# The first block's meta-token work and the last rows' normalization of a hybrid DeltaNet and attention layer, rewritten

## The chip, the cores and the metric

The kernel runs on one core of one Trainium2 chip. Its time is device microseconds (us) of one launch, and a kernel's time is the median of its runs. TensorE (PE in rows) does the matmuls; VectorE (DVE), ScalarE (ACT) and GpSimd (POOL) do elementwise work; SyncE (SP) issues nearly all transfers, in the order in which they are written. Each engine executes its own list of instructions in order and waits on semaphores for the others.

## What is computed

One layer over 2048 tokens of width 1024, preceded by 16 learned meta tokens. Cut to what matters:

```python
h = concatenate([meta, x], axis=1)
q_a, k_a, v_a, z_a, beta_a, dec_a, q_b, k_b, v_b, z_b, gate_a, gate_b = split(h @ w_in)
# branch A: gated DeltaNet, 8 heads of 128, chunks of 64
q, k, v = silu(causal_conv4(concat([q_a, k_a, v_a])))        # 4 taps a channel
beta = sigmoid(beta_a);  g = -exp(a_log) * softplus(dec_a + dt_bias)
lower = strict_tril(k_beta @ k.T * decay)
sol = triangular_solve(lower + eye, [v_beta, k_beta * exp(g_cum)])   # per chunk and head
S = S * exp(g_last) + k_dec.T @ (u - w @ S)                  # state carried over chunks
# branch B: sliding-window attention, 16 heads of 64, meta tokens always visible
mixed = sigmoid(gate_a) * (y_a @ w_proj_a) + sigmoid(gate_b) * (y_b @ w_proj_b)
out = layer_norm(alpha * x + mixed @ w_out)                  # rows of the 16 meta tokens dropped
```

## The kernel before

The 2048 tokens are four blocks of 512. A block runs through a fixed list of projections with weights of 128 output columns (a "unit", 24 matmuls of 128x512, `proj`, line 296), and between the pieces of six matmuls a loop (`run`) draws the next step of two side streams: the DeltaNet stages of the head groups and the attention. What an engine executes, and in which order, is so decided when the program is built, by counting those pieces ("ticks"); steps put off with `bg` come a written number of ticks later. On the chip each engine then goes through its list as soon as the semaphores allow.

Each fp32 matrix is split into a high part (rounded by ScalarE, line 261) and a low part (raw minus high, `split_lo`, line 144), and three products are summed. From the second block on, many high and low parts are read back from a DRAM copy that the first block wrote (`ws`), so the splitting is mostly work of block 0.

The eight DeltaNet heads run in four groups of two (g0 to g3). For each group and chunk the triangular system is inverted in two levels. The 32x32 diagonal blocks are inverted column by column on GpSimd: 31 columns of two instructions each (lines 812 and 814), on `X`, with `g` the transposed lower matrix. SP then stores `X` (line 820), loads it transposed as `XT` (line 825), GpSimd copies it into place (line 828), and TensorE's first matmuls that need it are those of line 890 (`XN`), which join the blocks. The four groups do this one after another; SP's list holds the store of `X` between the stores of weight parts (line 283) and the loads of the next weights (line 248).

In block 0 alone the 16 meta tokens run along: `meta_tok` makes their gates with `gates_math`, a second call of it beside that of the block's tokens; `meta_heads` gives each group its start state. It convolves the meta tokens' keys and values with four taps (`meta_conv`, lines 403 and 405), and inverts a 16x16 matrix per head, 15 columns of two instructions on two partitions (lines 472 and 474). All of this is on VectorE. The inversion stands in the same stretch of the program as the columns of lines 812 and 814.

Attention (`ls`, `mn`: lines 1077 to 1110) follows the DeltaNet groups. The last block ends with the output projection and, row tile by row tile (four of 128 tokens), with `sums` (line 1303: residual plus PSUM), `stats` (line 1306) and `norm_row`: line 1287 aggregates mean and variance, `rsqrt_small` (lines 160 to 166) makes the root with three Newton steps of three instructions, ScalarE applies it (line 1293), and weight and bias are applied on GpSimd, for the last row tile on VectorE (lines 1297 and 1298).

## Time and profile before

| | |
|---|---|
| median of 3 runs | 2669.69 us (2668.91 to 2675.93) |
| the profiled execution | 2665.94 us |
| its span, first to last instruction | 2664.2 us |
| mean granted TensorE clock | 0.994 |
| PE busy | 2600.1 us (98%) |
| DVE busy | 1587.5 us (60%) |
| ACT busy | 1223.7 us (46%) |
| POOL busy | 765.8 us (29%) |
| DMA, mean over the span | 173 GB/s |

Busy time is a sum over an engine's instructions. TensorE is busy nearly all the time, so the few stretches in which it waits, and what stands before its first and behind its last matmul, are what is left beside the matmuls themselves. All rows below are of the profiled execution, whose time is 1.74 us above its span.

### The profile page before, as it was taken

To read this page: it belongs to the slowest core of one execution; us is meant where nothing else is said; L and a number is where in the kernel's file an instruction comes from. 1 tells how busy PE (TensorE), PEld (TensorE's weight loads), DVE (VectorE), ACT (ScalarE), POOL (GpSimd) and SP (SyncE) were. 2 spreads that over 40 slices of the span, in tenths; PEclk is the share of its full clock that TensorE was granted. 3 is DMA by queue.
4 is the path that set the end of the run, shared out by engine and by line. 5 is a ranking of instruction groups with operands and counts; after the bars stand their busy time and mean duration, and the time that the engine had idled before them with its cause. 6 is when DMAs were issued, how large, how long until landed. Compare 5 with 4: busy or idle time off the path is not lost.

```text
span 2664.2 us, 44181 instructions
## 1 busy us (share of the span) xinstructions
PE 2600.1 (98%) x15308; PEld 2180.1 (82%) x15308; DVE 1587.5 (60%) x4041; ACT 1223.7 (46%) x3250; POOL 765.8 (29%) x1703
## 2 busy tenths in 40 slices
PE   8999999999999999999999999999999999999997
PEld 7677778888888888888887888888888788888885
DVE  6879758743565655762465564774347466476336
ACT  4556546542244545662224553664223455465422
POOL 2544324432055430111116433110103644011022
PEclk9999999999999999999999999999999999999998
DMA  7654555643574454664466445575357544567533
GB/s 256 203 175 165 186 193 187 197 164 97 196 250 147 144 168 149 206 196 142 152 219 194 147 138 159 179 210 179 114 165 247 158 146 149 159 193 213 166 95 126
DMA packets 243376, 461.64 MB, mean 173 GB/s; under 512 B 77993, under 2 KB 136001, under 8 KB 243153
## 3 DMA queue, kind: packets, MB, share of 16 engines
q1 hardware_dynamic: 243152, 458.82, 54.2%
q8 instruction: 121, 1.98, 0.3%
q14 instruction: 103, 0.84, 0.1%
HBM read 379.89 MB, written 78.82 MB: 172 GB/s over the span
## 4 chain that ended last, share of the span: by engine, by line
PE 81%; DVE 10%; DMA 3%; POOL 2%; ACT 2%; issue 1%; SPq 1%; DVEq 0%; POOLq 0%; ACTq 0%
PE acc L296 57%; PE ps L1110 2%; DVE s L689 2%; PE ps L1075 2%; PE ps L962 1%; PE ps L941 1%; PE ps L949 1%; PE ps L951 1%; PE ps L930 1%; PE ps L1128 1%; PE acc L1367 1%; PE acc L1370 1%; PE acc L1369 1%; PE ps L841 1%; POOL X L814 1%
## 5 line engine op out<-in xcount | busy, mean ns | idle before, releaser
L296 PE MATMUL acc<-xh,wh 128*128 128x512 f32 x1800 | 738.0, 410 | 1.7 <-ACT wh L261 1.7
L296 PE MATMUL acc<-xl,wh 128*128 128x512 f32 x1800 | 709.4, 394 | 0.0
L296 PE MATMUL acc<-xh,wl 128*128 128x512 f32 x1800 | 476.2, 396 | 0.0
L296 PEld LDWEIGHTS acc<-xh,wh 128*128 128x128 f32 x1800 | 341.2, 190 | 62.3 <-ACT wh L261 2.4
L296 PEld LDWEIGHTS acc<-xl,wh 128*128 128x128 f32 x1800 | 342.0, 190 | 58.1
L296 PEld LDWEIGHTS acc<-xh,wl 128*128 128x128 f32 x1800 | 331.2, 189 | 67.3 <-issue 0.5
L261 ACT ACTIVATE wh<-wr 128x1024 fp32r<-128x1024 f32 (+1 forms) x245 | 258.0, 1053 | 276.0 <-PE acc L296 162.9
L689 DVE SCALAR_TENSOR_TENSOR s<-st,cw,s 128x512 f32<-128x512 f32 x288 | 233.4, 810 | 66.6 <-ACT st L684 59.5
L144 DVE TENSOR_TENSOR wl<-wr,wh 128x1024 fp32r<-128x1024 f32 (+2 forms) x125 | 162.0, 1296 | 156.5 <-ACT wh L261 137.5
L296 PE MATMUL acc<-y,wh 128*128 128x512 f32 x1024 | 250.1, 392 | 0.0
L812 POOL TENSOR_TENSOR tm<-X,g 128x60 f32<-128x60 f32 (+24 forms) x496 | 167.3, 337 | 268.8 <-DMA g<-d 233.4
L296 PEld LDWEIGHTS acc<-y,wh 128*128 128x128 f32 x1024 | 189.1, 188 | 37.3
L296 PE MATMUL acc<-xh,wr 128*128 128x512 f32 x624 | 209.0, 402 | 0.0
L1227 POOL TENSOR_TENSOR g<-g 128x512 f32<-128x512 f32 x32 | 69.9, 2183 | 432.7 <-DVE g L1220 432.7
L814 POOL TENSOR_TENSOR X<-X,tm 128x60 f32<-128x60 f32 (+24 forms) x496 | 165.4, 333 | 38.9
L1220 DVE SCALAR_TENSOR_TENSOR g<-g,acc 128x512 f32<-128x512 f32 x64 | 44.0, 688 | 203.3 <-PE acc L296 203.1
L1056 POOL TENSOR_TENSOR g<-mo,slp 128x32 f32<-128x32 f32 x128 | 41.0, 330 | 389.7 <-DVE mn L1077 365.3
L1112 ACT ACTIVATE s<-ps 104x512 fp32r<-104x512 f32 (+2 forms) x128 | 76.4, 597 | 146.6 <-PE ps L1110 145.6
L296 PEld LDWEIGHTS acc<-xh,wr 128*128 128x128 f32 x624 | 116.2, 188 | 23.0
L1211 ACT ACTIVATE g<-acc,bg__157 128x512 f32<-128x512 f32 x64 | 44.1, 689 | 190.3 <-PE acc L296 189.7
L296 PE MATMUL acc<-y,wl 128*128 128x512 f32 x512 | 129.2, 391 | 0.0
L731 POOL TENSOR_TENSOR g<-cm,gh 128x256 fp32r<-128x256 f32 x64 | 50.7, 822 | 257.8 <-DVE gh L643 211.5
(327 smaller groups left out, 4761.5 us busy)
## 6 DMA issues: line engine op xcount, KB each, us to landing
wr<-in_wfm_dram SPq DMA_DIRECT2D x214, 512.0 KB
wl<-ws SPq DMA_DIRECT2D x165, 512.0 KB
wr<-ws SPq DMA_DIRECT2D x78, 512.0 KB
wh<-ws SPq DMA_DIRECT2D x75, 512.0 KB
ws<-wl SPq DMA_DIRECT2D x68, 512.0 KB
g<-kd SPq DMA_DIRECT2D x240, 96.0 KB
ws<-wh SPq DMA_DIRECT2D x38, 512.0 KB
wr<-in_wo_dram SPq DMA_DIRECT2D x32, 512.0 KB
```

Of the source, the lines that this page charges most:

```text
L144: eng.tensor_tensor(out=out_, in0=src, in1=f(hi), op=ALU.subtract)
L261: A.activation(hi, raw, AF.Copy)
L296: T.matmul(ps, w_[:, k, :], r_(k), start=(n == 0), stop=(n == 3 * NK - 1))
L689: V.scalar_tensor_tensor(out=acc, in0=st[:, 3 - d:TB + 3 - d], scalar=cw[:, s, 3 - d:4 - d], in1=acc, op0=ALU.mult, op1=ALU.add)
L731: G.tensor_tensor(out=gt[:, hh, c:c + 2], in0=tri.unsqueeze(1).to_broadcast([P, 2, P]), in1=part[:, c:c + 2, h0 + hh:h0 + hh + 1].to_broad ...
L812: G.tensor_tensor(out=tm[:, :n, :r], in0=X[:, :n, j:j + 1].to_broadcast([P, n, r]), in1=L[:, j:j + 1, j + 1:].to_broadcast([P, n, r]), op= ...
L814: G.tensor_tensor(out=X[:, :n, j + 1:], in0=X[:, :n, j + 1:], in1=tm[:, :n, :r], op=ALU.add)
L1075: T.matmul(o_, d["q", rt][:, 2 * cp2 + ch], KX[:, l, ch, s:208], start=l == 0, stop=l == 1)
L1110: T.transpose(out=pT[0:kt, j * 256 + rt * P:j * 256 + rt * P + P], in_=Pt[:, ch, rt, s + j * kt:s + j * kt + kt], identity=ident)
L1112: A.activation(ph[0:kt], pT[0:kt], AF.Copy)
L1211: A.activation(gt_[u][:, br, :], ps, AF.Tanh, scale=0.5, bias=bg_[:, 8 * br + u:8 * br + u + 1])
L1227: G.tensor_tensor(out=m[:, u % 2, :], in0=t[:, 0, :], in1=t[:, 1, :], op=ALU.add)
```

## The change

Five things are rewritten; what is computed stays the same.

- The gates of the meta tokens become a fifth column of the block's gate tile in block 0: one call of `gates_math` on five columns takes the place of two calls. Its polynomial takes 9 instructions in place of 17, in all blocks.
- The four taps of the meta tokens (7 instructions a call, 8 calls) and their inversion columns (30 instructions a group) go from VectorE to GpSimd.
- A low part that GpSimd makes (30 in block 0) is made in four pieces of 128x256.
- The first tile of x and the first weights are loaded and rounded in two pieces each.
- Roots: `rsqrt_col`, for one value per partition, takes two instructions a Newton step, with the operands as per-partition scalars. `norm_row` gives GpSimd fewer columns from row tile to row tile, and VectorE the others in two fused instructions; the last row tile's second half is multiplied by the weight before the root is there.

```diff
@@ -140,8 +140,11 @@
 
     f = lambda ap: ap.bitcast(F32)
     def split_lo(out_, src, hi, pool=False):
-        eng = G if pool else V
-        eng.tensor_tensor(out=out_, in0=src, in1=f(hi), op=ALU.subtract)
+        if not pool:
+            V.tensor_tensor(out=out_, in0=src, in1=f(hi), op=ALU.subtract)
+            return
+        for k in range(0, NK, 2):
+            G.tensor_tensor(out=out_[:, k:k + 2], in0=src[:, k:k + 2], in1=f(hi[:, k:k + 2]), op=ALU.subtract)
 
     S = [cp.tile([P, 2, P], F32, name=f"S{g}") for g in range(4)]
     carry = cp.tile([P, 24, 3], F32, name="carry")
...
@@ -153,17 +156,27 @@
-    def rsqrt_small(dst, x, shp, tag):
-        hx = tiny(shp, tag + "h")
+    def rsqrt_seed(dst, x, shp, tag):
         it = tp.tile(shp, I32, tag=tag + "i", name=nm(tag + "i"))
-        t = tiny(shp, tag + "t")
         V.tensor_scalar(out=it, in0=x.bitcast(I32), scalar1=1, scalar2=None, op0=ALU.logical_shift_right)
         V.tensor_scalar(out=dst.bitcast(I32), in0=it, scalar1=-1.0, scalar2=MAGIC, op0=ALU.mult, op1=ALU.add)
+        return tiny(shp, tag + "t")
+
+    def rsqrt_small(dst, x, shp, tag):
+        t = rsqrt_seed(dst, x, shp, tag)
+        for _ in range(3):
+            V.scalar_tensor_tensor(out=t, in0=x, scalar=-0.5, in1=dst, op0=ALU.mult, op1=ALU.mult)
+            V.tensor_tensor(out=t, in0=t, in1=dst, op=ALU.mult)
+            V.scalar_tensor_tensor(out=dst, in0=t, scalar=1.5, in1=dst, op0=ALU.add, op1=ALU.mult)
+
+    def rsqrt_col(dst, x, tag):
+
+        t = rsqrt_seed(dst, x, [P, 1], tag)
+        hx = tiny([P, 1], tag + "h")
         V.tensor_scalar(out=hx, in0=x, scalar1=-0.5, scalar2=None, op0=ALU.mult)
         for _ in range(3):
-            V.tensor_tensor(out=t, in0=dst, in1=dst, op=ALU.mult)
-            V.tensor_tensor(out=t, in0=t, in1=hx, op=ALU.mult)
-            V.scalar_tensor_tensor(out=dst, in0=t, scalar=1.5, in1=dst, op0=ALU.add, op1=ALU.mult)
+            V.tensor_scalar(out=t, in0=dst, scalar1=dst, scalar2=hx, op0=ALU.mult, op1=ALU.mult)
+            V.tensor_scalar(out=dst, in0=t, scalar1=1.5, scalar2=dst, op0=ALU.add, op1=ALU.mult)
 
 
     wlist, on_pool = weight_order(nblk)
...
@@ -341,11 +356,9 @@
         z = tiny(shp, sg + "z")
         V.tensor_tensor(out=z, in0=t, in1=t, op=ALU.mult)
         pl = tiny(shp, sg + "pl")
-        V.tensor_scalar(out=pl, in0=z, scalar1=2.0 / 17, scalar2=2.0 / 15, op0=ALU.mult, op1=ALU.add)
-        for c in (13, 11, 9, 7, 5, 3, 1):
-            V.tensor_tensor(out=pl, in0=pl, in1=z, op=ALU.mult)
-            V.tensor_scalar(out=pl, in0=pl, scalar1=2.0 / c, scalar2=None, op0=ALU.add)
-        V.tensor_tensor(out=pl, in0=pl, in1=t, op=ALU.mult)
+        V.tensor_scalar(out=pl, in0=z, scalar1=2.0 / 17, scalar2=None, op0=ALU.mult)
+        for c in (15, 13, 11, 9, 7, 5, 3, 1):
+            V.scalar_tensor_tensor(out=pl, in0=pl, scalar=2.0 / c, in1=z if c > 1 else t, op0=ALU.add, op1=ALU.mult)
         V.scalar_tensor_tensor(out=pl, in0=u, scalar=0.0, in1=pl, op0=ALU.max, op1=ALU.add)
         gg = tiny(shp, sg + "g")
         V.tensor_tensor(out=gg, in0=pl, in1=expa[:pr].unsqueeze(1).to_broadcast(shp), op=ALU.mult)
...
@@ -355,31 +368,30 @@
 
     meta = {}
 
-    def meta_tok(psm):
+    def meta_tok(psm, ba):
 
         ms = s2([32, 272])
         V.tensor_copy(ms, psm[:32, :272])
-        yield 4
+        yield 2
         pf = bank()
         T.matmul(pf[:NM, :272], i2, ms, start=True, stop=True)
+        V.tensor_copy(ba[:NM, NC4, :], pf[:NM, 256:272])
         vm = s2([NM, KV, 2, 64], F32R)
         pv = pf[:NM, :256].rearrange("p (k d) -> p k d", k=KV)
         A.activation(vm[:, :, 0, :], pv, AF.Copy)
         V.tensor_tensor(out=vm[:, :, 1, :], in0=pv, in1=f(vm[:, :, 0, :]), op=ALU.subtract)
-        bm = tiny([NM, 1, 16], "bm")
-        V.tensor_copy(bm[:, 0, :], pf[:NM, 256:272])
-        yield 1
+        r = {}
+        yield from gates_math(ba, NC4 + 1, P, r)
         SY.dma_start(out=vd[0:NM], in_=f(vm))
-        r = {}
-        yield from gates_math(bm, 1, NM, r)
-        yield 2
+        bk = cp.tile([NM, 2, NH], F32, name="bgm")
+        V.tensor_copy(bk[:, 0, :], r["b"][:NM, NC4, :])
+        V.tensor_copy(bk[:, 1, :], r["g"][:NM, NC4, :])
+        meta["blk"] = r["b"][:, 0:NC4, :], r["g"][:, 0:NC4, :]
+        yield 3
         pe = bank()
-        T.matmul(pe[:NM, :NH], strict[:NM, :NM], r["g"][:, 0, :], start=True, stop=True)
+        T.matmul(pe[:NM, :NH], strict[:NM, :NM], bk[:, 1, :], start=True, stop=True)
         es = cp.tile([NM, NH], F32, name="esm")
         A.activation(es, pe[:NM, :NH], AF.Exp)
-        bk = cp.tile([NM, 2, NH], F32, name="bgm")
-        V.tensor_copy(bk[:, 0, :], r["b"][:, 0, :])
-        V.tensor_copy(bk[:, 1, :], r["g"][:, 0, :])
         meta["b"], meta["g"], meta["es"] = bk[:, 0, :], bk[:, 1, :], es
 
     def meta_kb(u):
...
@@ -400,9 +412,9 @@
         tmp = tiny([P, 2, NM], "mtmp")
         for tap in range(4):
             wv = cw[:, base:base + 2, tap].unsqueeze(2).to_broadcast([P, 2, NM])
-            V.tensor_tensor(out=tmp if tap else acc, in0=mstage[:, 2 * kind:2 * kind + 2, tap:tap + NM], in1=wv, op=ALU.mult)
+            G.tensor_tensor(out=tmp if tap else acc, in0=mstage[:, 2 * kind:2 * kind + 2, tap:tap + NM], in1=wv, op=ALU.mult)
             if tap:
-                V.tensor_tensor(out=acc, in0=acc, in1=tmp, op=ALU.add)
+                G.tensor_tensor(out=acc, in0=acc, in1=tmp, op=ALU.add)
         yield 2
         th = tiny([P, 2, NM], "mth")
         A.activation(th, acc, AF.Tanh, scale=0.5)
...
@@ -469,9 +481,9 @@
         yield 4
         for j in range(NM - 1):
             n, r = j + 1, NM - 1 - j
-            V.tensor_tensor(out=tm[:, :n, :r], in0=X[:, :n, j:j + 1].to_broadcast([2, n, r]),
+            G.tensor_tensor(out=tm[:, :n, :r], in0=X[:, :n, j:j + 1].to_broadcast([2, n, r]),
                             in1=L[:, j:j + 1, j + 1:].to_broadcast([2, n, r]), op=ALU.mult)
-            V.tensor_tensor(out=X[:, :n, j + 1:], in0=X[:, :n, j + 1:], in1=tm[:, :n, :r], op=ALU.add)
+            G.tensor_tensor(out=X[:, :n, j + 1:], in0=X[:, :n, j + 1:], in1=tm[:, :n, :r], op=ALU.add)
             if j % 5 == 4:
                 yield 2
         yield 1
...
@@ -504,15 +516,24 @@
 
         xh, xl = dst
         raw = y4([P, 2, TB])
-        SY.dma_start(out=raw, in_=xT[:, 2 * q:2 * q + 2, b * TB:(b + 1) * TB])
+        ks = (slice(0, 1), slice(1, 2)) if b == q == 0 else (slice(0, 2),)
+        src = xT[:, 2 * q:2 * q + 2, b * TB:(b + 1) * TB]
+        for k in ks:
+            SY.dma_start(out=raw[:, k], in_=src[:, k])
+            if len(ks) > 1 and k is ks[0]:
+                next_dma()
         if lag:
             yield lag
         h = xp.tile([P, 2, TB], F32R, tag="x", name=nm("xh"))
-        A.activation(h, raw, AF.Copy)
-        if lag:
-            yield 2
         l = xp.tile([P, 2, TB], F32R, tag="x", name=nm("xl"))
-        split_lo(l, raw, h)
+        for k in ks:
+            A.activation(h[:, k], raw[:, k], AF.Copy)
+            if lag:
+                yield 2
+            split_lo(l[:, k], raw[:, k], h[:, k])
+            if len(ks) > 1 and k is ks[0]:
+                for _ in next_split():
+                    pass
         xh.append(h)
         xl.append(l)
 
...
@@ -606,10 +625,17 @@
                             yield
 
             def end():
-                ba = tiny([P, NC4, 16], "ba")
+                if first:
+                    ba = cp.tile([P, NC4 + 1, 16], F32, name="ba0")
+                    V.memset(ba[:, NC4, :], 0.0)
+                else:
+                    ba = tiny([P, NC4, 16], "ba")
                 for c in range(NC4):
                     V.tensor_copy(ba[:, c, :], accs[c][:, 256:272])
-                bg(gates_math(ba, NC4, P, gates))
+                if first:
+                    bg(meta_tok(psm, ba))
+                else:
+                    bg(gates_math(ba, NC4, P, gates))
                 vs = []
                 for c in range(NC4):
                     vst = s2([P, KV, 2, 64], F32R)
...
@@ -624,11 +650,12 @@
                     SY.dma_start(out=vd[NM + t0 + c * P:NM + t0 + (c + 1) * P], in_=f(vst))
 
             bg(end())
+            yield
+
+        def decays():
             if first:
-                bg(meta_tok(psm))
-            yield
-
-        def decays():
+                yield from until(lambda: "blk" in meta)
+                gates["b"], gates["g"] = meta.pop("blk")
             yield from until(lambda: "g" in gates)
             gdec = gates["g"]
             pe = bank()
...
@@ -1283,19 +1305,35 @@
 
             def norm_row(c, params):
                 lw, lb = params
+                end_row = c == NC4 - 1
+                n = 512 if end_row else 256 * c
+                own, rest = slice(0, n), slice(n, D)
+                x0, x1 = (xr[c][:, sl] for sl in (own, rest))
                 mv = tiny([P, 1, 2], "mvr")
                 V.bn_aggr(out=mv[:, 0, :], in_=bss[c])
-                rs = scale(1, mv)
+                mean = mv[:, 0, 0:1]
                 nmr = tiny([P, 1], "nmr")
-                V.scalar_tensor_tensor(out=nmr, in0=mv[:, :, 0], scalar=-1.0, in1=rs, op0=ALU.mult, op1=ALU.mult)
-                for h in range(2):
-                    sl = slice(512 * h, 512 * h + 512)
-                    A.activation(xr[c][:, sl], xr[c][:, sl], AF.Identity, scale=rs, bias=nmr)
-                for h in range(2):
-                    sl = slice(512 * h, 512 * h + 512)
-                    E_ = V if c == NC4 - 1 else G
-                    E_.tensor_tensor(out=xr[c][:, sl], in0=xr[c][:, sl], in1=lw[:, sl], op=ALU.mult)
-                    E_.tensor_tensor(out=xr[c][:, sl], in0=xr[c][:, sl], in1=lb[:, sl], op=ALU.add)
+                if end_row:
+                    V.tensor_scalar(out=nmr, in0=mean, scalar1=-1.0, scalar2=None, op0=ALU.mult)
+                    A.activation(x1, x1, AF.Identity, scale=1.0, bias=nmr)
+                    G.tensor_tensor(out=x1, in0=x1, in1=lw[:, rest], op=ALU.mult)
+                var = tiny([P, 1], "var")
+                V.tensor_scalar(out=var, in0=mv[:, 0, 1:2], scalar1=16.0 * LN_EPS, scalar2=None, op0=ALU.add)
+                rs = tiny([P, 1], "lrs")
+                rsqrt_col(rs, var, "ln")
+                if not end_row:
+                    V.tensor_scalar(out=nmr, in0=mean, scalar1=rs, scalar2=-1.0, op0=ALU.mult, op1=ALU.mult)
+                    A.activation(x1, x1, AF.Identity, scale=rs, bias=nmr)
+                    for sl in (slice(n, 512), slice(max(n, 512), D)):
+                        if sl.stop > sl.start:
+                            G.tensor_tensor(out=xr[c][:, sl], in0=xr[c][:, sl], in1=lw[:, sl], op=ALU.mult)
+                            G.tensor_tensor(out=xr[c][:, sl], in0=xr[c][:, sl], in1=lb[:, sl], op=ALU.add)
+                if n:
+                    V.scalar_tensor_tensor(out=x0, in0=x0, scalar=mean, in1=lw[:, own], op0=ALU.subtract, op1=ALU.mult)
+                    V.scalar_tensor_tensor(out=x0, in0=x0, scalar=rs, in1=lb[:, own], op0=ALU.mult, op1=ALU.add)
+                if end_row:
+                    V.scalar_tensor_tensor(out=x1, in0=x1, scalar=rs, in1=lb[:, rest], op0=ALU.mult, op1=ALU.add)
+                for sl in (slice(0, 512), slice(512, D)):
                     SY.dma_start(out=out_[t0 + c * P:t0 + (c + 1) * P, sl], in_=xr[c][:, sl])
 
             def sums(c, half, acc):
```

What it moves on the engines' lists, at three places. In an order row stand the line, the operation, what it writes and reads, and the shape; `x4` is four in a row. The change's line numbers are higher: 812 and 814 are 839 and 841, 472 and 474 are 484 and 486, 745 is 772, 820 is 847, 825 is 852, 248 is 262, 283 is 298.

GpSimd, within the columns of group g0 (`X_1013`), before:

```order
L812 TENSOR_TENSOR tm_1015<-X_1013,g_882 128x28
L814 TENSOR_TENSOR X_1013<-X_1013,tm_1015 128x28
L745 TENSOR_TENSOR g_1020<-g_1020,cm 128x512
L812 TENSOR_TENSOR tm_1015<-X_1013,g_882 128x2x27
L814 TENSOR_TENSOR X_1013<-X_1013,tm_1015 128x2x27
L812 TENSOR_TENSOR tm_1015<-X_1013,g_882 128x2x26
L814 TENSOR_TENSOR X_1013<-X_1013,tm_1015 128x2x26
L745 TENSOR_TENSOR g_1020<-g_1020,cm 128x512
```

and now (`g_968` holds the two meta matrices):

```order
L839 TENSOR_TENSOR tm_1015<-X_1013,g_924 128x28
L841 TENSOR_TENSOR X_1013<-X_1013,tm_1015 128x28
L772 TENSOR_TENSOR g_1020<-g_1020,cm 128x512
L484 TENSOR_TENSOR g_968<-g_968 2x15
L486 TENSOR_TENSOR g_968<-g_968 2x15
L484 TENSOR_TENSOR g_968<-g_968 2x2x14
L486 TENSOR_TENSOR g_968<-g_968 2x2x14
L484 TENSOR_TENSOR g_968<-g_968 2x3x13
L486 TENSOR_TENSOR g_968<-g_968 2x3x13
```

The block's columns stay in their order; behind the fourth of them now stand 10 of the meta tokens' column instructions (six are shown), 20 more between later columns, and one group of seven taps further on.

SP, around the store of `X` of g0, before:

```order
L248 DMA wr_1399<-in_wfm_dram 128x1024
L820 DMA d_251_1412<-X_1013 256x1x32 x4
L482 DMA mXT_1433<-md_239_1360 16x2x16
L825 DMA XT_1456<-d_251_1412 32x8x32 x4
L283 DMA ws_1461<-wh_1370 128x1024
L283 DMA ws_1462<-wl_1372 128x1024
L248 DMA wr_1494<-in_wfm_dram 128x1024
```

and now:

```order
L262 DMA wr_1369<-in_wfm_dram 128x1024
L847 DMA d_244_1384<-X_1013 256x1x32 x4
L852 DMA XT_1422<-d_244_1384 32x8x32 x4
L298 DMA ws_1427<-wh_1340 128x1024
L298 DMA ws_1428<-wl_1342 128x1024
L262 DMA wr_1461<-in_wfm_dram 128x1024
```

The store of `X` and the load of `XT` stay next to each other, ahead of the next weight load; the transposed load of the meta matrix (`mXT`) has moved ahead of them.

VectorE, the last row tile's normalization at the end of the kernel, before (behind `rsqrt_small`):

```order
L164 TENSOR_TENSOR lnt_27874<-lrs_27871 128x1
L165 TENSOR_TENSOR lnt_27874<-lnt_27874,lnh_27872 128x1
L166 SCALAR_TENSOR_TENSOR lrs_27871<-lnt_27874,lrs_27871 128x1
L1290 SCALAR_TENSOR_TENSOR nmr_27887<-mvr_27867,lrs_27871 128x1
L1297 TENSOR_TENSOR y_27506<-y_27506,y_27662 128x512
L1298 TENSOR_TENSOR y_27506<-y_27506,y_27664 128x512
L1297 TENSOR_TENSOR y_27506<-y_27506,y_27662 128x512
L1298 TENSOR_TENSOR y_27506<-y_27506,y_27664 128x512
```

and now (from the last Newton step on):

```order
L178 TENSOR_SCALAR lnt_27821<-lrs_27817,lnh_27822 128x1
L179 TENSOR_SCALAR lrs_27817<-lnt_27821,lrs_27817 128x1
L178 TENSOR_SCALAR lnt_27821<-lrs_27817,lnh_27822 128x1
L179 TENSOR_SCALAR lrs_27817<-lnt_27821,lrs_27817 128x1
L1332 SCALAR_TENSOR_TENSOR y_27458<-y_27458,mvr_27809,y_27614 128x512
L1333 SCALAR_TENSOR_TENSOR y_27458<-y_27458,lrs_27817,y_27616 128x512
L1335 SCALAR_TENSOR_TENSOR y_27458<-y_27458,lrs_27817,y_27616 128x512
```

The root's three-instruction steps are steps of two, all with scalar operands, and the four 128x512 instructions behind the root are three, none of which waits for ScalarE's pass over the whole row.

## Rows read from the trace of the kernel before

**Rows 1.** The page: busy time of TensorE, its share of the span, its instructions.

```profile
PE 2600.1 (98%) x15308; PEld 2180.1 (82%) x15308; DVE 1587.5 (60%) x4041; ACT 1223.7 (46%) x3250; POOL 765.8 (29%) x1703
```

**Rows 2.** TensorE's waits in block 0 (0 to 721 us): total us, times, longest.

```profile
PE ps L762 <- DVE g L694: 7.9, 3, 3.5
PE acc L600 <- ACT wh L261: 6.7, 1, 6.7
PE ps L859 <- ACT g L861: 5.5, 2, 2.8
PE ps L1110 <- DVE g L1096: 4.2, 6, 1.3
...
PE ps L492 <- issue: 1.2, 1, 1.2
PE ps L900 <- ACT Y L895: 0.9, 2, 0.8
```

**Rows 3.** Groups of VectorE instructions in block 0: busy us, mean ns, idle before.

```profile
L474 DVE TENSOR_TENSOR g<-g 2x15 f32<-2x15 f32 (+7 forms) x60 | 16.2, 270 | 2.1
L472 DVE TENSOR_TENSOR g<-g 2x15 f32<-2x15 f32 (+7 forms) x60 | 15.8, 264 | 1.7
L1091 DVE TENSOR_TENSOR ls<-ls,m 128x4 f32<-128x4 f32 x16 | 14.2, 889 | 0.0
```

**Rows 4.** Groups of GpSimd instructions in block 0, the same columns.

```profile
L812 POOL TENSOR_TENSOR tm<-X,g 128x60 f32<-128x60 f32 (+24 forms) x124 | 49.2, 397 | 98.7 <-DMA g<-d 90.0
L814 POOL TENSOR_TENSOR X<-X,tm 128x60 f32<-128x60 f32 (+24 forms) x124 | 41.9, 338 | 9.7
```

**Rows 5.** Timeline of GpSimd, group g3's first columns: start us, duration us.

```profile
308.13 0.24 POOL L812 TENSOR_TENSOR tm<-X,g 128x31 f32<-128x31 f32 x1 [32.82 <-DMA g<-d]
...
309.41 0.24 POOL L812 TENSOR_TENSOR tm<-X,g 128x29 f32<-128x29 f32 x1
```

**Rows 6.** Timeline, g0: last column, store of X, last copies, TensorE's first use.

```profile
110.35 0.72 POOL L814 TENSOR_TENSOR X<-X,tm 128x8 f32<-128x8 f32 x1
111.10 2.68 SPq L820 DMA_DIRECT2D d<-X  x4
118.92 2.39 POOL L828 COPY g<-XT 32x256 f32<-32x256 f32 x3 [0.38 <-DMA XT<-d]
130.69 0.69 PE L890 MATMUL ps<-XN,g 32*32 32x32 f32 x32
```

**Rows 7.** Timeline, g1, g2, g3: last column and TensorE's first use.

```profile
178.99 0.22 POOL L814 TENSOR_TENSOR X<-X,tm 128x8 f32<-128x8 f32 x1
...
201.10 0.66 PE L890 MATMUL ps<-XN,g 32*32 32x32 f32 x30
...
261.39 0.22 POOL L814 TENSOR_TENSOR X<-X,tm 128x8 f32<-128x8 f32 x1
...
283.89 0.64 PE L890 MATMUL ps<-XN,g 32*32 32x32 f32 x16
...
339.92 0.22 POOL L814 TENSOR_TENSOR X<-X,tm 128x8 f32<-128x8 f32 x1
...
355.71 0.69 PE L890 MATMUL ps<-XN,g 32*32 32x32 f32 x32
```

**Rows 8.** Timeline of the end: VectorE's sums of the row tiles, TensorE's last matmuls.

```profile
2631.94 0.67 DVE L1303 SCALAR_TENSOR_TENSOR y<-y,ps 128x512 f32<-128x512 f32 x1
...
2636.01 0.68 DVE L1303 SCALAR_TENSOR_TENSOR y<-y,ps 128x512 f32<-128x512 f32 x1
...
2645.02 0.61 PE L1367 MATMUL ps<-g,y 128*128 128x512 f32 x2
...
2645.58 1.26 POOL L1298 TENSOR_TENSOR y<-y,y 128x512 f32<-128x512 f32 x1
2645.72 1.14 DVE L165 TENSOR_TENSOR lnt<-lnt,lnh 128x1 f32<-128x1 f32 x1
...
2650.30 0.68 DVE L1303 SCALAR_TENSOR_TENSOR y<-y,ps 128x512 f32<-128x512 f32 x1
...
2660.40 0.69 DVE L1298 TENSOR_TENSOR y<-y,y 128x512 f32<-128x512 f32 x1
```

More of the change, by code (lines that the diff above doesn't have):

```diff
@@ L247, in next_dma @@
             raw = wp.tile(shape, F32, tag="wr", name=nm("wr"))
-            SY.dma_start(out=raw, in_=src)
+            for k in ((slice(0, 1), slice(1, 3)) if i == 0 else (slice(None),)):
+                SY.dma_start(out=raw[:, k], in_=src[:, k])
             raws[i] = (raw, shape)
@@ L260, in next_split @@
         hi = g4(shape, F32R) if keep else wp.tile(shape, F32R, tag="wh", name=nm("wh"))
-        A.activation(hi, raw, AF.Copy)
+        for k in ((slice(0, 1), slice(1, 3)) if i == 0 else (slice(None),)):
+            A.activation(hi[:, k], raw[:, k], AF.Copy)
         lo = g4(shape, F32R) if keep else wp.tile(shape, F32R, tag="wl", name=nm("wl"))
@@ L323, in gates_math @@
         shp = [pr, n, NH]
-        sg = f"gm{n}"
+        sg = "gm"
         be = tiny(shp, sg + "be")
@@ L506, in load_x @@
         raw = y4([P, 2, TB])
-        SY.dma_start(out=raw, in_=xT[:, 2 * q:2 * q + 2, b * TB:(b + 1) * TB])
+        ks = (slice(0, 1), slice(1, 2)) if b == q == 0 else (slice(0, 2),)
+        src = xT[:, 2 * q:2 * q + 2, b * TB:(b + 1) * TB]
+        for k in ks:
+            SY.dma_start(out=raw[:, k], in_=src[:, k])
+            if len(ks) > 1 and k is ks[0]:
+                next_dma()
         if lag:
@@ L523, in hybrid_kernel @@
             pass
-        if q < 2:
+        if q == 1:
             next_dma()
@@ L528, in hybrid_kernel @@
             SY.dma_start(out=xmr, in_=xmT)
-            for _ in next_split():
-                pass
         if q == 1:
@@ L626, in tokens @@
             bg(end())
-            if first:
-                bg(meta_tok(psm))
             yield
         def decays():
+            if first:
+                yield from until(lambda: "blk" in meta)
+                gates["b"], gates["g"] = meta.pop("blk")
             yield from until(lambda: "g" in gates)
@@ L1260, in norm_params @@
                 return lw, lb
-            def scale(n, mv):
-                var = tiny([P, n], "var")
-                V.tensor_scalar(out=var, in0=mv[:, :, 1], scalar1=16.0 * LN_EPS, scalar2=None, op0=ALU.add)
-                rs = tiny([P, n], "lrs")
-                rsqrt_small(rs, var, [P, n], "ln")
-                return rs
             def norm():
@@ L1274, in norm @@
                     V.bn_aggr(out=mv[:, c, :], in_=bss[c])
-                rs = scale(NC4, mv)
+                var = tiny([P, NC4], "var")
+                V.tensor_scalar(out=var, in0=mv[:, :, 1], scalar1=16.0 * LN_EPS, scalar2=None, op0=ALU.add)
+                rs = tiny([P, NC4], "lrs")
+                rsqrt_small(rs, var, [P, NC4], "ln")
                 for c in range(NC4):
```

## The prediction

> **What bounds the kernel now.** I read the page first: TensorE is busy 2600.1 of 2664.2 us [rows 1], so only the 64 us in which it stands still can be won, and every new wait of TensorE costs its full length. The list of its waits says where they are. In block 0 it waits 6.7 us for the first weights, 7.9 us in three pieces and 5.5 us in two for VectorE and ScalarE in the front of the DeltaNet groups, 4.2 us in six for attention's VectorE work, then 1.2 and 0.9 us [rows 2]. The rest is the end: the last matmuls end at 2645.02 + 0.61 = 2645.63 us and VectorE's last instruction at 2660.40 + 0.69 = 2661.09 [rows 8]. So two places decide: the end, and block 0, where the change takes work off VectorE and lays it on GpSimd. That GpSimd is busy only 29% of the span is an average and says nothing of the stretch in question, where it inverts matrices for which TensorE has to wait if they come late.
>
> **The cover that the moved columns use up.** In g0 GpSimd's last column ends at 110.35 + 0.72 = 111.07, SP stores X at once (111.10), and the copies end at 118.92 + 2.39 = 121.31: 10.2 us from the last column until TensorE could go on. It takes up X only at 130.69, so 9.4 us are to spare [rows 6]. The same 10.2 us behind the last columns of g1, g2 and g3 (ended 179.21, 261.61, 340.14) give 189.4, 271.8 and 350.4 against first uses at 201.10, 283.89 and 355.71: 11.7, 12.0 and 5.3 us to spare [rows 7]. Together 38.4 us.
>
> **What is laid on that path.** 30 meta column instructions a group, and in g0 a tap group of seven, stand between the block's own columns in GpSimd's list. No row of before shows them on GpSimd, so their price is bounded from both sides. Below: GpSimd's smallest columns with nothing in their way, four in 309.41 - 308.13 = 1.28 us, or 0.32 us each [rows 5]. Above: the mean over all 248 column instructions of block 0, busy 49.2 + 41.9 and idle beside the transfer wait 8.7 + 9.7, so 109.5 / 248 = 0.44 us [rows 4]. On VectorE the same columns take 264 to 270 ns each [rows 3]. The tiles are small (15 to 64 elements a partition) like the first ones, but other VectorE work runs beside them, as in the mean: I take the middle, 0.38 us, and keep both ends. A group's columns then cost c = 30 x 0.38 = 11.4 us, the taps 7 x 0.38 = 2.7 us.
>
> A rule speaks against this move. The row says that a column instruction of GpSimd takes 338 to 397 ns where VectorE's takes 264 to 270, 1.4 times as long on tiles of about the same width [rows 3, 4]. The Trainium skill, GPSIMD Engine Reference, section "Elementwise — side-by-side cycle accounting", measures the same kind of operation at 1.96 times VectorE's time on 2048 elements and keeps elementwise work on VectorE; by that factor a moved column would take an estimated 0.52 us, a group 15.7 us, and the sum below would be +14.6 us in place of -2.6.
>
> **How late TensorE comes.** X of g0 is late by 11.4 + 2.7 - 9.4 = 4.7 us, and TensorE with it. The start of each next group hangs on TensorE's earlier matmuls, so the delay is handed on: g1 4.7 + 11.4 - 11.7 = 4.4, g2 4.4 + 11.4 - 12.0 = 3.8, g3 3.8 + 11.4 - 5.3 = 9.9 us. In general 4c + 2.7 - 38.4 = 4c - 35.7. The waits for VectorE and ScalarE ahead of these points (7.9 and 5.5 us [rows 2]) may well go, with the second gate call, the taps and the columns off VectorE; but they are no term of their own, because whoever comes sooner to a late X waits there. That holds as long as the delay stays above what TensorE wins: in g1 at most 2.8 us of one wait off 4.7 leaves 1.9, below 4.4; in g2 at most 2.8 + 3.5 us. X binds in all four. The X store's place in SP's list adds to it: a late X holds the store of weight parts and the next weight load behind it; since TensorE stands still in the same time, I add nothing for this.
>
> **Behind the groups.** The waits of 1.2 and 0.9 us [rows 2] stand behind g3's use, where what they wait for will have come when TensorE is 9.9 us late: -2 us. Low parts in four pieces: VectorE's 128x4 instructions of line 1091 take 889 ns each [rows 3], far above their size, as long as a GpSimd instruction runs beside them; shorter pieces let them in sooner, and part of the 4.2 us behind attention's VectorE work goes: -2, bounds 0 and -4.2. GpSimd has slack there, so the extra instructions cost nothing.
>
> **The start.** Rounding the first tiles in halves can shorten the wait of 6.7 us [rows 2]; I set 0, since the next tile of x comes no sooner and TensorE reaches it earlier, with -2 us (an estimate, a third of that wait) as the bound.
>
> **The end.** VectorE needs 2636.01 - 2631.94 = 4.07 us for the first row tile, but (2650.30 - 2636.01) / 2 = 7.15 for each of the next two, since instructions of one element a partition with two tensor operands take 1.14 us while GpSimd's of 1.26 us run [rows 8]. The new root has scalar operands only and is not of this kind. Of 4.07 us two instructions of 0.68 are sum and statistics; the rest is some fourteen small ones, about 0.19 each. Three fall away: 3.5 us a row tile. VectorE is then through with three at 2631.94 + 10.5 us, and with the fused instructions of row tiles 1 and 2 (two of 128x256, two of 128x512 at 0.69) at 2644.5, before the last matmul. The last row tile ends at 2645.63 + 3.5 + 3 x 0.72 = 2651.3 in place of 2661.1: 9.8 us. Those three fused instructions have two tensor operands; GpSimd still has its share of row tiles 2 and 3 to do, and held by three instructions of 1.26 us the gain is 6.0. I take one hold: -8.5.
>
> **Sum.** 9.9 - 2 - 2 + 0 - 8.5 = -2.6 us, or T = 4c - 48.2. The profiled execution would go from 2665.94 to 2663.3; it lay 3.75 us under the median of the runs shown, so the median goes from 2669.69 to 2667.1.
>
> **Rivals.** A measurement of this kernel can tell about 0.3%, 8 us, from no change. In T that is reached at c = 10.05 (0.335 us a column) downwards and c = 14.05 (0.468 us) upwards.
>
> - *The columns are cheap.* At the lower bound, c = 9.6, T = -9.8: 2659.9 us. For it: VectorE, whose instructions hold GpSimd's as GpSimd's hold its, loses 60 + 60 column instructions in just this stretch [rows 3], so GpSimd's own columns may speed up too, which makes room. Should X not bind at all, the 7.9 and 5.5 us count as well. Chance 0.37.
> - *GpSimd becomes the bound and the kernel slower.* The place is TensorE's first use of X in each group, the price four times what a column costs over its cover, the point 0.468 us a column. At 0.52 T = +14.6: 2684.3 us. For it: the mean of 0.44 is near, a group's columns wait for each other, and g3 has only 5.3 us to spare. Against it: the unhindered 0.32. Chance 0.19. The Trainium skill's factor of 1.96 (GPSIMD Engine Reference, the section above) is the case for this one; the trace's ratio of 1.4 bears it out only in part.
> - *The middle*, columns between these points, -8 to +8 us: 0.44, and the forecast. A smaller gain at the end (6.0) or none from the low parts leaves T at most 4.5 us higher, within this case. Its own range is 2662 to 2675.
>
> **How the numbers follow.** The likeliest case gives 2667.1. Low end: c = 9.6 with the end unheld (-1.3), the start's 2 and the low parts' other 2.2 us, -15.3: 2654. High end: 0.48 us a column, c = 14.4, T = +9.4, and half a microsecond for the delayed weight loads: 2680. Chances: faster 0.37, same 0.44, slower 0.19.
>
> **What would show it.** Right: a wait of TensorE at line 917 (the new number of 890) in each group, released by GpSimd's copies of XT, with the first use of X in g3 near 365.6 us; the end of g0's columns some 14 us later against its start than before; the waits for line 694's result shrunk; last matmul to last instruction some 8.5 us shorter. Wrong: no wait at line 917, that is, columns well under 0.32 us or an earlier start of the chain (then faster by more than 10 us); or columns at half a microsecond, with weight loads late behind the X store (slower).

## The result, and the profile after

The median went from 2670.15 us (four runs) to 2694.67 us (three runs); the ratio to the kernel before is 1.0085 (95% interval 1.0062 to 1.0109). A fourth run of the changed kernel, slow at a granted clock of 0.751, took 3231.21 us and is left out. The change made the kernel slower, by 23 to 25 us, where 2667.1 us and a range up to 2680 were forecast. The profiled execution took 2696.41 us, its span 2694.6.

The page, first line:

```profile
PE 2616.5 (97%) x15308; PEld 2194.1 (81%) x15308; DVE 1518.1 (56%) x3764; ACT 1224.4 (45%) x3246; POOL 835.2 (31%) x1968
```

VectorE lost 69 us of work and GpSimd gained 69, as meant [rows 1]. TensorE's busy time grew by 16.4 us although its 15308 instructions are the same. Its waits in block 0 (0 to 760 us), beside [rows 2]:

```profile
PE ps L789 <- DVE g L721: 29.5, 3, 14.3
PE acc L329 <- ACT s L326: 4.7, 2, 4.1
PE acc L619 <- ACT wh L276: 4.6, 1, 4.6
PE ps L886 <- DVE g L959: 3.8, 2, 1.9
PE ps L917 <- DVE XN L904: 3.4, 1, 3.4
...
PE ps L1137 <- DVE g L1123: 0.5, 2, 0.3
```

The waits for the convolution's result (line 721, before 694) are not gone but grew from 7.9 to 29.5 us. Two of the three places are the same (in g0 and g2, 3.5 and 2.5 us before, 14.3 and 8.9 now); the third, 6.3 us in g1, is new, and the wait of 1.9 us early in the block is gone. Line 917, where X was to be waited for, shows one wait of 3.4 us. The start's wait fell from 6.7 to 4.6 us, and attention's from 4.2 to 0.5 us.

What held line 721 in g0 is seen on the timelines of ScalarE, VectorE, TensorE and SP, from 92 to 124 us (start, duration, and in brackets the idle time before and who ended it):

```profile
92.58 0.33 SPq L262 DMA_DIRECT2D wr<-in_wfm_dram  x1
110.11 0.24 SPq L491 DMA_DIRECT2D md<-g  x1
...
113.40 0.64 SPq L262 DMA_DIRECT2D wr<-in_wfm_dram  x1
...
121.26 0.23 ACT L420 ACTIVATE mth<-macc 128x32 f32<-128x32 f32 x1 [16.24 <-POOL macc L417]
121.40 1.06 ACT L276 ACTIVATE wh<-wr 128x1024 fp32r<-128x1024 f32 x1
...
123.01 0.77 DVE L721 SCALAR_TENSOR_TENSOR g<-s,s 128x512 f32<-128x512 f32 x1 [1.30 <-ACT s L719]
123.83 0.47 PE L789 MATMUL ps<-cm,g 128*128 128x128 f32 x1 [14.28 <-DVE g L721]
```

Two lists stand still at once. SP waits with the store of the inverted meta matrix (line 491) for GpSimd's columns, and the next weight load, behind it, goes out at 113.40, 20.8 us after the one before. ScalarE stands 16.2 us at the tanh of the taps (line 420), which GpSimd reaches only behind the columns. The rounding of the weights (line 276) and the convolution's tanh (line 719) are behind that, then VectorE's line 721 and TensorE's line 789.

In g1 and g2 it is the store of X (line 847) that stands in SP's list until the columns end, with the weight load behind it. In g1, where the columns end at 203.70:

```profile
203.73 2.97 SPq L847 DMA_DIRECT2D d<-X  x4
...
207.91 0.74 SPq L262 DMA_DIRECT2D wr<-in_wfm_dram  x1
...
213.65 1.06 ACT L276 ACTIVATE wh<-wr 128x1024 fp32r<-128x1024 f32 x1 [5.62 <-DMA wr<-in_wfm_dram]
...
216.10 1.09 PE L789 MATMUL ps<-cm,g 128*128 128x128 f32 x4 [6.33 <-DVE g L721]
```

The weight load before this one went out at 192.88, 15.0 us earlier.

The last columns and TensorE's first uses of X, beside [rows 6, 7]:

```profile
127.93 0.22 POOL L841 TENSOR_TENSOR X<-X,tm 128x8 f32<-128x8 f32 x1
143.45 0.69 PE L917 MATMUL ps<-XN,g 32*32 32x32 f32 x32
...
203.48 0.22 POOL L841 TENSOR_TENSOR X<-X,tm 128x8 f32<-128x8 f32 x1
219.68 0.53 PE L917 MATMUL ps<-XN,g 32*32 32x32 f32 x12
...
294.94 0.22 POOL L841 TENSOR_TENSOR X<-X,tm 128x8 f32<-128x8 f32 x1
316.44 0.69 PE L917 MATMUL ps<-XN,g 32*32 32x32 f32 x32
...
382.00 0.22 POOL L841 TENSOR_TENSOR X<-X,tm 128x8 f32<-128x8 f32 x1
390.25 0.69 PE L917 MATMUL ps<-XN,g 32*32 32x32 f32 x32 [3.45 <-DVE XN L904]
```

The columns end 17.1, 24.5, 33.6 and 42.1 us later than before, TensorE's use comes 12.8, 18.6, 32.6 and 34.5 us later.

Two stretches around the wait of g0, by the view of stretches (length, then busy us of PE, PEld, DVE, ACT, POOL, then the granted clock, DMA share and GB/s):

```profile
109.00:124.00 15.00, 0.72 (x13) 0.47 (x4) 1.18 (x3) 2.74 (x7) 12.02 (x43) 0.58 0.69 246
124.00:130.00 6.00, 6.00 (x21) 4.85 (x22) 3.12 (x5) 3.02 (x15) 3.68 (x7) 0.64 0.04 5
```

A long wait is paid for once more: in the 6 us after it TensorE is busy throughout at a clock of 0.64, most of the time at its lower level of 1.2 GHz. From its first matmul to that of block 1, block 0 takes 40.5 us more (755.0 for 714.5): TensorE stands still 50.2 us in place of 26.8 and is busy 704.8 us in place of 687.6, with the same matmuls. An estimate of what the clock costs, from slices of 2 us: busy time times what the granted clock lacks of 1 comes to 21.2 us in this block, 5.1 before. These 16.1 us are nearly all of the 17.1 us by which TensorE was busy longer, and over a third of the block's loss.

The end, beside [rows 8], first TensorE's last matmuls on the timeline:

```profile
2681.71 0.61 PE L1405 MATMUL ps<-g,y 128*128 128x512 f32 x2
```

and the groups of VectorE from 2668 us on (count, then busy us and mean ns, idle before):

```profile
L178 DVE TENSOR_SCALAR lnt<-lrs,lnh 128x1 f32<-128x1 f32 x12 | 3.3, 273 | 0.4
L1332 DVE SCALAR_TENSOR_TENSOR y<-y,mvr,y 128x512 f32<-128x512 f32 (+1 forms) x3 | 3.0, 994 | 0.0
...
L179 DVE TENSOR_SCALAR lrs<-lnt,lrs 128x1 f32<-128x1 f32 x12 | 2.6, 215 | 0.4
```

From the last matmul's end to the end of the span it is 2694.6 - 2682.3 = 12.3 us, before 18.6: a gain of 6.3 us. No root instruction is held by GpSimd any more, but with two scalar operands they take 0.27 and 0.21 us.

### The profile page after: what moved, and what is told of

Its sections match the earlier page's. It is cut to its first block, busy times and chain, and to the rows that moved or that the text cites. A ratio compares the mean times of both kernels' runs of the same rounds, so it can differ in the third digit from the quotient of the medians.

```text
span 2694.6 us, 44178 instructions
## 1 busy us (share of the span) xinstructions
PE 2616.5 (97%) x15308; PEld 2194.1 (81%) x15308; DVE 1518.1 (56%) x3764; ACT 1224.4 (45%) x3246; POOL 835.2 (31%) x1968
## 3 DMA queue, kind: packets, MB, share of 16 engines
q8 instruction: 121, 1.98, 0.3%
## 4 chain that ended last, share of the span: by engine, by line
PE 61%; DVE 3%; POOL 2%; DMA 2%; ACT 1%; issue 1%; SPq 1%; DVEq 0%; POOLq 0%; ACTq 0%
PE acc L311 43%; PE ps L1137 2%; PE ps L1102 1%; POOL X L841 1%; POOL tm L839 1%; PE ps L978 1%; PE ps L968 1%; PE ps L976 1%; PE ps L957 1%; PE ps L989 1%; PE ps L1155 1%; DVE s L716 1%; PE acc L1405 1%; PE acc L1407 1%; PE acc L1408 1%; PE ps L868 1%
## 5 line engine op out<-in xcount | busy, mean ns | idle before, releaser
L147 POOL TENSOR_TENSOR wl<-wr,wh 128x256 fp32r<-128x256 f32 x120 | 89.4, 776 | 134.4 <-ACT wh L276 104.4
```

The costliest lines, as they stand in the source:

```text
L147: G.tensor_tensor(out=out_[:, k:k + 2], in0=src[:, k:k + 2], in1=f(hi[:, k:k + 2]), op=ALU.subtract)
```

## The experiments

Two theories stood after the first comparison. A: the taps on GpSimd hold ScalarE. B: the columns on GpSimd make X late, and with it the weight loads behind its store. After e1 to e3 a third was split off. C: the columns hold SP, and the weight loads behind it are the loss; from there on B is the lateness of X alone. Ratios are to the kernel before, run on the same chip, with 95% intervals. In the diffs `-` is the changed kernel's line, unless another is named.

**e1, taps back on VectorE.**

```diff
-            G.tensor_tensor(out=tmp if tap else acc, in0=mstage[...], in1=wv, op=ALU.mult)
+            V.tensor_tensor(out=tmp if tap else acc, in0=mstage[...], in1=wv, op=ALU.mult)
-                G.tensor_tensor(out=acc, in0=acc, in1=tmp, op=ALU.add)
+                V.tensor_tensor(out=acc, in0=acc, in1=tmp, op=ALU.add)
```

> The changed kernel with only the meta taps back on VectorE; the inversion columns stay on GpSimd. Theory A (ScalarE's tanh of the taps stands at the head of its list and waits until GpSimd has come through the columns that stand ahead of the taps; all of ScalarE's later work and so VectorE's and TensorE's is held): the 16.2 us and 7.1 us waits of ScalarE for the taps are gone, TensorE's wait of 14.3 us in group g0 falls below 4 us, and the kernel takes 2670 to 2680 us. Theory B (only the lateness of X and of the weight loads queued behind its store costs time): the taps are 7 of 69 instructions of one chain, X of g0 comes 2 to 3 us sooner, and the kernel takes 2686 to 2694 us.

Measured 2688.54 us, 1.0082 (1.0063 to 1.0101), in B's range; the changed kernel's ratio of 1.0085 lies within the interval, so the taps alone cost nothing that can be measured here. Not A alone. ScalarE's wait for the taps is gone and another stands in its place; the timelines of SP, ScalarE and TensorE in g0:

```profile
111.44 0.24 SPq L491 DMA_DIRECT2D md<-g  x1
...
119.80 1.06 ACT L276 ACTIVATE wh<-wr 128x1024 fp32r<-128x1024 f32 x1 [13.35 <-DMA wr<-in_wfm_dram]
122.20 1.12 PE L789 MATMUL ps<-cm,g 128*128 128x128 f32 x4 [11.28 <-DVE g L721]
```

TensorE goes on at 122.20 where it was 123.83.

**e2, columns back on VectorE** (`G.` to `V.` in the two lines 484 and 486; taps on GpSimd).

> The changed kernel with only the meta inversion columns back on VectorE; the taps stay on GpSimd. Theory A: the 30 columns of 0.36 us ahead of the taps are gone, so ScalarE's wait of 16.2 us falls to about 5 us and does not vanish, and 2668 to 2678 us. Theory B: X is on time in all groups, no weight load is late behind its store, TensorE's waits in block 0 are those of before or fewer, 2658 to 2664 us.

Measured 2658.73 us, 0.9965 (0.9953 to 0.9977). The columns are the cause; without them the change is faster than the kernel before. TensorE's largest wait left is 9.2 us for a weight, while SP waits 11.8 us at line 491 for VectorE's columns: with the gates in one call that store stands one weight load earlier in SP's list. That the one comes from the other was the reading then; k6 below refutes it.

**e3, both back.**

> The changed kernel with the taps and the columns both back on VectorE; gates, roots, ends, pieces as in the change. Both theories: no ScalarE wait for the taps and X on time; what is left is the gain of the other edits, the end 6.3 us and 0 to 8 us of block 0: 2655 to 2664 us. If a third cause lies in the gates as a fifth column or in the pieces, it stays above 2664 us.

Measured 2659.21 us, 0.9961 (0.9948 to 0.9974), as e2: beside the columns the taps cost nothing of their own.

**e4, roots, end and polynomial alone, on the kernel before.**

> The kernel before with only the new roots, the new end and the shorter gate polynomial. The last matmul to last instruction takes 12.3 us as in the changed kernel in place of 18.6, so 2662 to 2665 us by both theories; near 2669 if the end's gain is lost elsewhere.

Measured 2657.56 us, 0.9962 (0.9947 to 0.9977), below the range expected. The gain is more than the 6 us of the end; in the profiled execution block 0 is 2.6 us shorter too.

**k1, e1 with the meta store issued by GpSimd.**

```diff
-        SY.dma_start(out=d2, in_=X)
+        G.dma_start(out=d2, in_=X)
```

> As e1 (taps on VectorE, columns on GpSimd), and the store of the inverted meta matrix is issued by GpSimd, behind its columns, in place of SP. Theory C (SP goes through its list in order; the store of line 491 waits there for GpSimd's columns and holds the next weight loads, for whose rounding ScalarE and then VectorE and TensorE wait): SP's 34.0 us of waits at line 491 are gone, ScalarE's wait of 13.4 us for a weight load in g0 falls below 5, TensorE's wait of 11.3 us in g0 below 4, and the kernel takes 2666 to 2680 us; the stores of X still hold SP in g1 to g3. Theory B (X comes late, and TensorE must wait for it wherever it stands): the wait moves to line 917, 2684 to 2692 us.

Measured 2697.87 us, 1.0111 (1.0089 to 1.0134), above both ranges. SP now stands at the next rows of its list that hang on the columns: 18.2 us at the load of what was stored (line 494), and at the store of X 44.3 us in place of 28.4. The run took away one hold and not SP's standing still, so it did not test C.

**k0, the changed kernel with that store issued by GpSimd.**

> The changed kernel (taps and columns on GpSimd) with only the store of the inverted meta matrix issued by GpSimd. If ScalarE's wait for the taps is a second hold beside SP's (theory A and C together), taking SP's away leaves it: ScalarE waits 12 us or more at line 420 in g0, TensorE 10 us or more there, and 2680 to 2694 us, at least 6 above the kernel with the taps on VectorE. If only SP's hold counts, both take the same, 2666 to 2680 us.

Measured 2695.71 us, 1.0104 (1.0089 to 1.0119), above both ranges. ScalarE waits 18.3 us at line 420 in g0, but the comparison with k1, meant to show the taps as a second hold, is undecided, since SP's hold was not gone in either.

**c1, the columns alone, on the kernel before** (lines 472 and 474, `V.` to `G.`).

> The kernel before with one edit: the meta inversion columns on GpSimd. By theory B and C the loss comes from these columns alone: slower than before by 12 to 30 us, 2681 to 2699 us, with SP waiting for GpSimd at line 479 and 820; in the old order the store of the meta matrix stands one weight load later, so its hold in g0 is shorter than the 17.4 us of the changed kernel. If the columns are harmless without the other edits, 2665 to 2672 us.

Measured 2703.56 us, 1.0136 (1.0121 to 1.0151): 36 us slower by this one edit, more than expected by any theory. TensorE waits at line 762 for line 694's result 32.9 us in four pieces, SP 26.3 us at the meta store and 25.0 at the store of X. No tap, gate or piece is needed for the loss.

**e8, all but the meta edits.** The diff of the change without its parts in `gates_math` (tag), `meta_tok`, `meta_conv`, `meta_heads`, `tokens` and `decays`.

> The changed kernel with all meta edits undone (gates in two calls, taps and columns on VectorE); roots, end, start pieces and low parts in four pieces stay. Against the kernel with ends and roots alone (2657.6 us) it shows start and pieces: theory of the prediction, -2 for the low parts and 0 to -2 for the start, 2653 to 2657 us. In the kernel with both back, TensorE waited 9.1 us in g0 for a weight load behind SP's line 491, which stands one load earlier there; with the old gates this wait should be below 2 us.

Measured 2655.79 us, 0.9952 (0.9936 to 0.9969); TensorE's long wait for a weight is not there. The 1.8 us between e8 and e4 are within the intervals, so the start and the low parts together are not shown as a gain.

**k3, e1 with all four transfers off SP:** store and load of the meta matrix (lines 491, 494) and of X (847, 852) issued by GpSimd in block 0.

```diff
-        SY.dma_start(out=d2, in_=X)
+        G.dma_start(out=d2, in_=X)
...
-                SY.dma_start(out=d2[:, :, :, q, :].rearrange("k s m i -> (k s) m i"), in_=X[32 * q:32 * q + 32])
+                (G if first else SY).dma_start(out=d2[:, :, :, q, :].rearrange("k s m i -> (k s) m i"), in_=X[32 * q:32 * q + 32])
```

> As e1 (columns on GpSimd, taps on VectorE), and in block 0 GpSimd issues all four transfers that hang on its columns: store and transposed load of the meta matrix, store and transposed load of X. SP then has nothing in its list that waits for the columns. Theory C (the loss is SP's list standing still and the weight loads behind it): ScalarE's waits for weight loads in block 0 go back from 68 to below 35 us, TensorE's waits at line 789 from 33 to below 12 us, and the kernel takes 2660 to 2674 us, at least 12 below e1. Theory B (X is late, whoever issues what): the waits move to line 917 and 2684 to 2700 us.

Measured 2687.52 us, 1.0076 (1.0058 to 1.0094). The time is B's. Both of C's first two numbers came true: ScalarE's waits for weight loads went to 32.8 us, TensorE's at line 789 to 2.7. The time did not come back, and TensorE's waits in block 0 show B's place for it:

```profile
PE ps L917 <- DVE XN L904: 18.6, 4, 5.1
PE ps L504 <- DMA mXT<-md: 7.1, 1, 7.1
...
PE ps L789 <- DVE g L721: 2.7, 2, 2.5
```

The last columns and TensorE's first uses of X in the same run:

```profile
131.31 0.22 POOL L841 TENSOR_TENSOR X<-X,tm 128x8 f32<-128x8 f32 x1
142.05 0.47 PE L917 MATMUL ps<-XN,g 32*32 32x32 f32 x10 [4.04 <-DVE XN L904]
...
204.96 0.72 POOL L841 TENSOR_TENSOR X<-X,tm 128x8 f32<-128x8 f32 x1
216.91 1.06 PE L917 MATMUL ps<-XN,g 32*32 32x32 f32 x32 [4.78 <-DVE XN L904]
...
296.57 0.22 POOL L841 TENSOR_TENSOR X<-X,tm 128x8 f32<-128x8 f32 x1
308.36 1.06 PE L917 MATMUL ps<-XN,g 32*32 32x32 f32 x32 [4.70 <-DVE XN L904]
...
376.81 0.22 POOL L841 TENSOR_TENSOR X<-X,tm 128x8 f32<-128x8 f32 x1
388.93 0.58 PE L917 MATMUL ps<-XN,g 32*32 32x32 f32 x14 [5.13 <-DVE XN L904]
```

With SP and ScalarE free TensorE runs into the late X itself, in all four groups. It uses X of g2 8 us sooner than in e1 and the changed kernel, but X of g3 only 0.8 and 1.3 us sooner. The transfers have a price of their own here: GpSimd spends 3.4 us on them in between the columns, and in g3 it takes 11.9 us from the last column to TensorE's use, where e1, with SP issuing, takes 7.9. So the run shows where TensorE stands once SP is free; what SP's hold costs by itself it does not show.

**k6, the same transfers on GpSimd, columns on VectorE.**

> The control to the run before: the same four transfers issued by GpSimd, but the columns on VectorE. It prices these transfers on GpSimd themselves. SP's wait of 11.8 us at line 491 and with it TensorE's 9.1 us wait in g0 should be gone: 2648 to 2657 us by theory C; above 2665 us if GpSimd's own waits for the transfers hold its later columns.

Measured 2658.55 us, 0.9968 (0.9957 to 0.9979), as e3, between the two ranges expected. So these transfers cost nothing while X has time to spare (TensorE has no wait at line 917 here); this does not price them in k3, where X is late. The 9 us wait for a weight in g0 stayed although SP no longer waits at line 491, and the timelines of VectorE, ScalarE and TensorE show what holds it:

```profile
97.53 0.36 DVE L486 TENSOR_TENSOR g<-g 2x60 f32<-2x60 f32 x1
97.82 0.15 DVE L161 TENSOR_SCALAR rsi<-sk 128x8 int32<-128x8 int32 x1
...
100.21 0.16 DVE L890 TENSOR_SCALAR sq<-sq 128x8 f32<-128x8 f32 x1
100.38 2.18 ACT L888 ACTIVATE g<-ps,irk 128x128 f32<-128x128 f32 x8 [5.88 <-DVE sq L890]
102.40 1.11 ACT L276 ACTIVATE wh<-wr 128x1024 fp32r<-128x1024 f32 x1
103.56 0.80 PE L311 MATMUL acc<-xh,wh 128*128 128x512 f32 x1 [8.96 <-ACT wh L276]
```

The rounding of the weight (line 276) stands in ScalarE's list behind line 888, which waits 5.9 us for a root on VectorE (lines 161 to 890). VectorE's list holds 20 of the meta columns' instructions ahead of that root; in e8, with the gates in two calls, the root is through at 93.7 and the columns begin at 96.3. From 96.0 to 102.4 us the DMA share is 0.00. So by this trace the hold that the fused gates bring is the order of VectorE's list, not SP's.

**k5, half of the columns:** the first 8 of 15 on GpSimd (`E_ = G if j < 8 else V`), taps on VectorE.

> As e1, but only the first 8 of the 15 meta columns on GpSimd, the last 7 on VectorE: 16 in place of 30 instructions a group in GpSimd's list. If the block's columns have cover (9.4, 11.7, 12.0 and 5.3 us by the trace of before) and the loss is what goes over it, 16 x 0.36 = 5.8 us a group stays under the cover and the kernel takes 2656 to 2666 us. If every moved column costs its time, half the loss of e1 against the kernel with both back (29 us) is left: 2671 to 2677 us.

Measured 2669.96 us, 1.0009 (0.9999 to 1.0018), between the two expectations: 16 of 30 instructions (53%) bring 10.8 of the 29.3 us (37%; by the ratios, as the runs are of two chips, 40%) that lie between e3 and e1. Less than in proportion, as with some cover, but not without cost.

**e9, e8 with the taps on GpSimd.**

> The fastest kernel so far (roots, end, start, pieces; 2655.8 us) with one more edit, the taps on GpSimd. If the taps on GpSimd hold ScalarE only because the moved columns stand ahead of them, it takes 2651 to 2658 us; if they hold it by themselves, in the middle of the block's own columns, ScalarE waits more than 5 us for them in g0 and 2659 to 2667 us.

Measured 2656.03 us, 0.9958 (0.9944 to 0.9972), as e8. ScalarE's one wait for the taps is 1.8 us: they hold it only where the moved columns stand ahead of them.

## Why the prediction was wrong

**The place was right, the cover was not.** The rival with GpSimd as the bound came true in sign, yet not by its condition: it wanted 0.468 us a column. In the changed kernel's block 0 the moved columns cost, by the groups of GpSimd (busy and mean ns, idle before):

```profile
L484 POOL TENSOR_TENSOR g<-g 2x15 f32<-2x15 f32 (+7 forms) x60 | 21.3, 356 | 3.8
L486 POOL TENSOR_TENSOR g<-g 2x15 f32<-2x15 f32 (+7 forms) x60 | 20.8, 346 | 4.7
```

That is (21.3 + 20.8 + 3.8 + 4.7) / 120 = 0.42 us, inside the bounds of 0.32 and 0.44. Put into 4c - 48.2 it gives +2.4 us, not +30. (The 0.52 us by the factor of 1.96 in the Trainium skill, GPSIMD Engine Reference, "Elementwise — side-by-side cycle accounting", is not borne out for tiles this small: 0.36 busy beside VectorE's 0.27 is 1.3 times.) The price was mis-sized by 5 us in all; that is not the step that failed.

**The step that failed** is "a late X holds the store of weight parts and the next weight load behind it; since TensorE stands still in the same time, I add nothing for this", and with it the 38.4 us of cover. The cover was counted from X to TensorE's first use of X. But SP's list, with the meta store ahead of weight loads and the store of X ahead of the next, ties the columns to the weights, which TensorE needs earlier: it stood still at line 789, ahead of line 917, and in g0 to g2 the work between the two then kept it until after X was there. By the rows, cover in use is the columns' lateness less TensorE's: 17.1 - 12.8 = 4.3 in g0 (I took 9.4), 5.9 in g1 (11.7), 1.0 in g2 (12.0), 7.6 in g3 (5.3), together 18.8 in place of 38.4. These 19.6 us are most of the 24.6 by which TensorE came later to X of g3 (34.5) than worked out (9.9).

The rest is seen when the first columns of each group are taken in as well. They start at 79.67, 147.89, 229.36 and 308.13 us before, at 84.62, 160.15, 246.09 and 340.07 in the changed kernel, at 85.28, 160.81, 246.95 and 334.49 in k3. TensorE's lateness at X of g3 is then the sum of four terms, in us:

| | predicted | changed kernel | k3 |
|---|---|---|---|
| later start of g0's columns | 0 | 5.0 | 5.6 |
| longer time from first to last column, four groups | 48.3 | 51.3 | 56.5 |
| handed on: later start of the next group's columns less TensorE's lateness | 0 | -3.0 | 5.2 |
| cover in use | -38.4 | -18.8 | -34.1 |
| TensorE's lateness at X of g3 | 9.9 | 34.5 | 33.2 |

(k3 has the taps on VectorE; without their 2.7 us the prediction's sum is 45.6 - 38.4 = 7.2.) Two things follow. With SP's hold gone the cover in use is nearly the one that I counted, 34.1 of 38.4; in e1, which differs from k3 only in who issues the four transfers, it is 19.6. So the count was right for a TensorE that waits only for X, and SP's list took half of it away. And k3 is nearly as late all the same, by three terms that the prediction had at nothing or too small: g0's columns start later, GpSimd needs longer from the first column to the last, and each delay is handed on larger than it came. The first comes with the fused gates: with the columns back on VectorE g0's columns start at 87.95 (e3), and with the old gates at 78.08 (e9). Of the second, 3.4 us are k3's own transfers. For the third the clock behind each wait is a likely cause, not shown apart from others: it was 0.50 in the slice of 4 us around each of the first three uses. How the 30 us of the changed kernel divide between the two holds, the lists and the late X, no run shows.

**Point by point.** "X binds in all four": right in k3, while in the changed kernel the lists ahead of it bound in g0, g1 and g2, and X only in g3. The columns' price: 0.42 for 0.38. "Behind the groups", -2 for late partners: wrong, TensorE still waited 2.3 us at line 927. Low parts, -2: attention's wait fell by 3.7 us, and by e8 that is no measurable gain in the whole. The start: 2.0 us less wait, at the bound given. The end: 6.3 for 8.5 us; row tile 1's two fused instructions of 128x256 took 1.5 and 1.4 us beside GpSimd's, and the root's instructions 0.21 to 0.27 us where 0.19 was taken. The sum misses a term of its own: the slower clock behind long waits, an estimated 16.1 us in block 0.

**The sum as measured,** from the two spans, 2694.6 - 2664.2 = +30.4 us: the start -2.0, block 0 +40.5, the other blocks -1.8, the end -6.3.

The rival of cheap columns, which got 0.37, was refuted by their price, 0.42 us, near the upper bound, and by e2 and c1: the loss comes from these columns alone. A group's whole chain of columns took 49 us in g2 and 42 in g3 for a reason beside the columns: these take 34.2 us in both, but g2's stretch of GpSimd's list holds two instructions of line 772, with 3.1 us of work and 5.5 us of waiting for ScalarE. The version without the meta edits, e8, beats both kernels.

## What to carry to other kernels

Before moving work to an engine with idle time, list for each moved instruction who waits for it, at which place of his own list, and what stands behind him: transfer queues and engines that execute in order pass a delay on to work that has nothing to do with it. Slack counted to the last consumer is only slack if no earlier entry of any such list waits for the same producer. When two holds run side by side, undoing one shows little about the other, and a remedy that loads the late engine further, as k3's transfers did, has a price of its own: the run that undid the producer told the cause, while the one that took the transfers away told only where TensorE stands next.

## What the runs showed of the hardware

Unlooked for was the price of a clock that falls: after a wait of 14.3 us TensorE worked 6 us at 0.64, with 8 matmuls of 128x512 taking 2.88 us together, where 8 of the same kind took 1.98 us ahead of the wait, at a granted clock of 1.00. And instructions with two per-partition scalar operands on one element took 0.27 and 0.21 us, against 0.16 for two tensor operands of the same size when not held.
